# The first gate product of a gated MLP on rows without their norm

## The chip, the core and the metric

The kernel runs on one NeuronCore of a Trainium2 chip. Its engines work side by side and meet at semaphores: TensorE (PE, with PEld for its weight loads), VectorE (DVE), ScalarE (ACT), GpSimd (POOL) and SyncE (SP, which issues the transfers). The metric is the time of one execution in microseconds on the device.

## The reference, cut to what matters

Two layers of a diffusion backbone on 256 latent and 256 context tokens with 2048 channels. Every sub-layer normalises its input, scales and shifts it by a vector that depends on the condition, and adds its result to the stream. The part at hand is the gated MLP of the second layer (layer 1), which follows that layer's attention and has 5504 inner channels:

```python
def rms_norm(x, g):
    xf = x.astype(jnp.float32)
    y = xf * lax.rsqrt(jnp.mean(xf * xf, axis=-1, keepdims=True) + NORM_EPS)
    return (y * g.astype(jnp.float32)).astype(x.dtype)

def modulate(x, shift, scale):
    return x * (1 + scale) + shift

def conv_ffn(u, w_gate, w_up, conv_w, conv_b, w_down):
    T = u.shape[1]
    gp = jnp.pad(u @ w_gate, ((0, 0), (1, 1), (0, 0)))
    gte = gp[:, :T] * conv_w[0] + gp[:, 1:T + 1] * conv_w[1] + gp[:, 2:] * conv_w[2] + conv_b
    return (jax.nn.silu(gte) * (u @ w_up)) @ w_down
```

Here u is the normalised, scaled and shifted stream. The norm's factor is one number per token, and the shift is one number per channel.

## The kernel before, in words

Channels lie on the 128 partitions, so the stream `hl` is 16 tiles (index k) of 128 channels by 256 tokens. Products run in 32-bit numbers held as a pair of a rounded high half and a low half. `split` makes such a pair of a weight piece: ScalarE casts the high half (L148), VectorE or GpSimd subtracts to get the low one (L150). The inner channels are 43 tiles (index f) of 128. A product of one f, g for the gate and u for the other factor, is 16 matmuls of 512 columns, high weights on the high and low rows side by side (L1018), and 16 matmuls of 256 columns, low weights on the high rows (L1021); they come in two halves of eight k. Each product fills one of four PSUM banks with the tag "gu". `gate1` reads the banks of g and u (ScalarE's copy at L1029 and VectorE's addition at L1030, which make `eg`), applies the convolution and the gate, and so frees them.

Ahead of it stands the attention's output (`_attention`): sixteen products `op0` to `op15` of the rows `oA0` to `oA15`, each added to `hl` (L1363). The function gives back the last of these additions; `hold` is a list of instructions behind which later splits are ordered.

The fourth norm `n4` is between the two. `add` squares each tile of `hl` on ScalarE (L347) and sums the squares on VectorE; `totals` sums over channels by matmuls with one column (`n4s`, L366) and reduces on VectorE (L369, L370); GpSimd takes the power (L374); `spread` puts the factors on a diagonal (`n4d`, VectorE L380) and spreads them over all partitions by one matmul (`n4b`, L382). Then `norm_b` makes the row pairs `B0` to `B15`: VectorE multiplies (`nrmB`, L986), ScalarE adds the shift and rounds the high half (L987), and the low half comes from VectorE for even k (L993), and from a second ScalarE operation (L990) and GpSimd (L991) for odd k. M(1, 4, k, 0) is the scale vector of tile k, M(1, 3, k, 0) the shift.

The order of the instructions on each engine is not written by hand. It comes from a simulation of the program when it is built, under priorities (`urgent`, `high_priority`) and the `hold` list; tiles come from pools with a fixed number of buffers, three and three for the weight pairs, and an instruction that takes a buffer waits for the last reader of the tile that had it before.

Of the kernel before, what the change touches and what calls it, by code (L numbers as in the profile page):

```python
# [10 lines left out]
F32 = mybir.dt.float32  # L11
F32R = mybir.dt.float32r
AF = mybir.ActivationFunctionType
ALU = mybir.AluOpType
AX = mybir.AxisListType
PSUM = bass.MemoryType.PSUM

P = 128
D = 2048
KT = D // P  # L20
T = 256
# [39 lines left out]
def kernel(ctx: ExitStack, tc: tile.TileContext, xT, cxT, wmod, wg, wu, wd, wp,  # L61
                         wq, wv, wo, vec, cc, rope, inv, strips, out):
    nc = tc.nc
# [16 lines left out]
    def flat(a):  # L80
        return a.rearrange("p s t -> p (s t)")
# [25 lines left out]
    hold = []  # L107
# [46 lines left out]
    def ld(src, name, share=0):  # L154
        return split(load(lambda a, b: src[:, a:b], 2048, name), name, share)
# [178 lines left out]
    class Norm:  # L334
# [8 lines left out]
        def add(self, h_of, k):  # L343
            sq = self.pool.tile([P, 512], F32, tag="t2", name=f"{self.name}q{k}")
            with self.urgent(k):
                for s in self.streams:
                    nc.scalar.activation(sq[:, T * s : T * s + T], h_of(s)[:, k, :], AF.Square)  # L347
                if k >= KT - self.ends:
                    self.last.append(sq)
                elif self.acc is None:  # L350
                    self.acc = sq
                else:
                    nc.vector.tensor_tensor(self.acc[:, : self.n], self.acc[:, : self.n], sq[:, : self.n], op=ALU.add)  # L353
# [22 lines left out]
        def spread(self, v, js, pb):  # L376

            dg = self.pool.tile([P, 512], F32, tag="t2", name=f"{self.name}d{js[0]}")
            for i, j in enumerate(js):
                nc.vector.tensor_scalar(dg[:, P * i : P * i + P], ident, v[:, j : j + 1], None, op0=ALU.mult)  # L380
            n = P * len(js)
            nc.tensor.matmul(pb[:, :n], ones, dg[:, :n], start=True, stop=True)  # L382
            return pb
# [60 lines left out]
    with ExitStack() as ph0:  # L444
# [6 lines left out]
        def h_of(s):  # L451
            return hc if s else hl
# [510 lines left out]

    for _ in moves:
        pass
    tail = _attention(tc, ap0, bank, ld, A, M, hl, wq, wv, wo, rope, band, ident, v_first)

    with ExitStack() as ph2:
        f1 = ph2.enter_context(tc.tile_pool(name="f1", bufs=8, reuse_waits="tile"))
# [6 lines left out]
        n4 = Norm((0,), f1, "n4", 2)  # L976
        for k in range(KT):
            n4.add(h_lat, k)
        rstd = n4.each()[0]
        B = {}  # L980

        def norm_b(ks):
            for k in ks:
                a = ap0.tile([P, 2, 2, T], F32R, tag=f"A{k}", name=f"B{k}")[:, 0]
                y = f1.tile([P, 512], F32, tag="t2", name=f"nrmB{k}")[:, 0:T]
                nc.vector.scalar_tensor_tensor(y, hl[:, k, :], M(1, 4, k, 0), rstd[:, 0:T], op0=ALU.mult, op1=ALU.mult)  # L986
                nc.scalar.activation(a[:, 0], y, AF.Identity, bias=M(1, 3, k, 0))  # L987
                if k % 2:
                    z = f1.tile([P, 512], F32, tag="t2", name=f"nrmBz{k}")[:, 0:T]
                    nc.scalar.activation(z, y, AF.Identity, bias=M(1, 3, k, 0))  # L990
                    nc.gpsimd.tensor_tensor(a[:, 1], z, a[:, 0].bitcast(F32), op=ALU.subtract)  # L991
                else:
                    ins = nc.vector.scalar_tensor_tensor(a[:, 1], y, M(1, 3, k, 0), a[:, 0].bitcast(F32),  # L993
                                                         op0=ALU.add, op1=ALU.subtract)
                B[k] = a
                if k == 9:
                    hold[:] = [ins.ins]

        def gu1(f):
            res = []  # L1000
            pre = None
            if f == 0:
                pre = [load(lambda a, b: w[1, f][:, a:b], 2048, f"w{nm}1_{f}") for nm, w in (("g", wg), ("u", wu))]
                for q, ts in enumerate(pre):
                    first = split(ts[:1], f"w{q}1_{f}_0")
                    hold[:] = [tail]
                    pre[q] = first + split(ts[1:], f"w{q}1_{f}_1")
                    hold.clear()
                norm_b(range(KT))
            elif f == 2:  # L1010
                hold.clear()
            for q, (nm, wsrc) in enumerate((("g", wg), ("u", wu))):
                parts = pre[q] if pre else ld(wsrc[1, f], f"w{nm}1_{f}", 2 if f % 4 > 1 else 0)
                ps = bank("gu", f"{nm}1_{f}")
                for j, (hi, lo) in enumerate(parts):
                    for k in range(8 * j, 8 * j + 8):
                        c = P * (k % 8)
                        nc.tensor.matmul(ps, hi[:, c : c + P], flat(B[k]), start=(k == 0), stop=False)  # L1018
                    for k in range(8 * j, 8 * j + 8):
                        c = P * (k % 8)  # L1020
                        nc.tensor.matmul(ps[:, T:], lo[:, c : c + P], B[k][:, 0], start=False, stop=(k == KT - 1))  # L1021
                res.append(ps)
            return res

        def gate1(f, banks):
            res = []
            for nm, ps in zip("gu", banks):
                e = f1.tile([P, 512], F32, tag="t2", name=f"e{nm}_{f}")[:, 0:T]
                nc.scalar.copy(e, ps[:, T:])  # L1029
                nc.vector.tensor_tensor(e, e, ps[:, :T], op=ALU.add)  # L1030
                res.append(e)
            pg, pu = res
            g1 = f1.tile([P, 512], F32, tag="t2", name=f"g1b_{f}")[:, 0:T]
            nc.scalar.activation(g1, pg, AF.Identity, scale=V("cw1_1")[:, f : f + 1], bias=V("cb_1")[:, f : f + 1])
            nc.vector.scalar_tensor_tensor(g1[:, 1:T], pg[:, 0 : T - 1], V("cw0_1")[:, f : f + 1],
                                           g1[:, 1:T], op0=ALU.mult, op1=ALU.add)
            nc.vector.scalar_tensor_tensor(g1[:, 0 : T - 1], pg[:, 1:T], V("cw2_1")[:, f : f + 1],
                                           g1[:, 0 : T - 1], op0=ALU.mult, op1=ALU.add)
            sg = f1.tile([P, 512], F32, tag="t2", name=f"sgb_{f}")[:, 0:T]
            nc.scalar.activation(sg, g1, AF.Silu)  # L1040
            nc.vector.tensor_tensor(sg, sg, pu, op=ALU.mult)
            a = f1.tile([P, 2, T], F32R, tag="act", bufs=8, name=f"actb_{f}")
            nc.scalar.copy(a[:, 0], sg)  # L1043
            nc.vector.tensor_tensor(a[:, 1], sg, a[:, 0].bitcast(F32), op=ALU.subtract)  # L1044
            return a
# [99 lines left out]
def _attention(tc, ap0, bank, ld, A, M, hl, wq, wv, wo, rope, band, ident, v_first):  # L1145
# [9 lines left out]
    with ExitStack() as es:  # L1155
# [179 lines left out]
                prev = v, P * j  # L1335
        queue.append(attend(KT - 1, *prev))

        X = {}

        def x_tile(k):  # L1340
            a = ap0.tile([P, 2, 2, T], F32R, tag=f"A{k}", name=f"oA{k}")[:, 0]
            nc.scalar.copy(a[:, 0], O[k])
            nc.vector.tensor_tensor(a[:, 1], O[k], a[:, 0].bitcast(F32), op=ALU.subtract)
            X[k] = a
# [41 lines left out]
        for m in range(KT):  # L1386
# [6 lines left out]
                o_mm(ps, parts, ks, m == KT - 1)  # L1393
            with tc.high_priority() if m == KT - 1 else ExitStack():
                ins = o_end(ps, m)
        return ins


# [97 lines left out]
```

## Time and profile before

| what | value |
|---|---|
| three timed runs | 3042.36, 3039.24, 3041.61 us; median 3041.61 |
| profiled execution | 3042.44 us, its span 3040.7 us |
| mean granted clock of TensorE | 0.991 |
| PE, PEld busy | 98%, 79% of the span |
| DVE, ACT, POOL busy | 68%, 44%, 29% |
| attention's output stage | about 2219 to 2294 us |
| fourth norm and the first rows | 2294 to 2302 us |
| layer 1's gated MLP | 2302 to 3030 us |

The times in the trace count from the span's start. A row of a timeline gives the start, the length, the engine and line, the operation with output and inputs, the shapes, the number of like instructions, and in brackets the idle time just before with what ended it. A row of waits gives the engine and line that waited, the one it waited for, the sum, the count and the longest. A row of windows gives the busy times of the engines in a stretch, TensorE's granted clock as a share of full speed, the share of the transfer engines, and GB/s.

### The profile page before, as it was taken

The page shows a single profiled execution, that of the slowest core. Times are in us where ns is not written, and L with a number is a line of the kernel's source. Part 1 is how long each engine was busy: PE and PEld are TensorE (multiplying, and loading weights), DVE is VectorE, ACT ScalarE, POOL GpSimd, SP SyncE. Part 2 cuts the span into 40 slices and gives each one's busy share as a digit, 9 for nine tenths or more (in the row PEclk, how much of TensorE's full clock was granted, in tenths as well). Part 3 has the DMA queues.
Part 4 walks back from the last instruction along what each step waited for, and adds up shares of the span by engine and source line. Part 5 has one row for each costly group of instructions (what it writes and reads, how often), then busy time and mean ns, then how long its engine had stood idle before and what let it go on. Part 6 is the DMA issues. An engine that isn't in the chain of part 4 may idle for free.

```text
span 3040.7 us, 40895 instructions
## 1 busy us (share of the span) xinstructions
PE 2972.1 (98%) x14846; PEld 2399.2 (79%) x14846; DVE 2054.5 (68%) x2894; ACT 1347.4 (44%) x2205; POOL 884.4 (29%) x868
## 2 busy tenths in 40 slices
PE   6999999999999999999999999999999999999998
PEld 2565678887888888888887888888888888888887
DVE  5445887576876867587686666474867666666666
ACT  3333473323334232333334444343546666566665
POOL 1111320303213030322413111010102566566665
PEclk9999999999999999999999999999999999999999
DMA  9878635454866857676783333333355555555563
GB/s 376 326 279 322 218 97 171 157 185 157 254 195 193 260 174 243 201 235 205 215 240 101 112 109 109 103 113 104 112 165 181 180 192 191 192 181 189 183 195 113
DMA packets 224778, 572.31 MB, mean 188 GB/s; under 512 B 55232, under 2 KB 68032, under 8 KB 224576
## 3 DMA queue, kind: packets, MB, share of 16 engines
q1 hardware_dynamic: 224576, 569.70, 58.0%
q8 instruction: 117, 1.92, 0.3%
q14 instruction: 85, 0.70, 0.1%
HBM read 563.32 MB, written 11.53 MB: 189 GB/s over the span
## 4 chain that ended last, share of the span: by engine, by line
PE 89%; issue 3%; DVE 3%; DMA 2%; ACT 1%; POOL 1%; SPq 0%; DVEq 0%; ACTq 0%; POOLq 0%
PE g L1018 5%; PE u L1018 5%; PE d L900 5%; PE d L902 5%; PE d L901 5%; PE d L1068 4%; PE u L865 4%; PE u L863 4%; PE u L864 4%; PE g L865 4%; PE g L864 4%; PE g L863 4%; PE u L1021 3%; PE g L1021 3%; PE d L1072 2%
## 5 line engine op out<-in xcount | busy, mean ns | idle before, releaser
L921 POOL TENSOR_TENSOR hl<-hl,dy 128x256 f32<-128x256 f32 x144 | 146.2, 1015 | 941.8 <-ACT dy L918 676.8
L1085 POOL TENSOR_TENSOR hl<-hl,dy 128x256 f32<-128x256 f32 x320 | 327.1, 1057 | 188.5 <-ACT dy L1083 186.2
L270 DVE SCALAR_TENSOR_TENSOR macc<-wm,sc,macc 128x512 f32<-128x512 f32 x360 | 262.3, 780 | 9.0 <-DMA wm<-wmod 8.9
L248 DVE SCALAR_TENSOR_TENSOR macc<-wm,sc,macc 128x1024 f32<-128x1024 f32 x120 | 160.4, 1336 | 87.3 <-DMA wm<-wmod 86.1
L918 ACT ACTIVATE dy<-d,modT 128x256 f32<-128x256 f32 x224 | 93.6, 471 | 138.6 <-PE d L902 134.7
L921 POOL TENSOR_TENSOR hc<-hc,dy 128x256 f32<-128x256 f32 x144 | 141.4, 982 | 0.0
L1261 POOL COPY bias<-rows 128x160 f32<-128x160 f32 x64 | 37.1, 579 | 306.2 <-issue 195.6
L1083 ACT ACTIVATE dy<-d,modT 128x512 f32<-128x512 f32 x160 | 104.5, 684 | 42.8 <-PE d L1072 41.3
L184 PE MATMUL mod<-wm,sc 128*32 128x512 f32 x640 | 101.6, 616 | 21.2 <-DVE n1q L353 18.9
L150 DVE TENSOR_TENSOR wd_2l<-wd,wd_2h 128x1024 fp32r<-128x1024 f32 (+1 forms) x44 | 58.6, 1343 | 60.5 <-ACT wd_2h L148 60.5
L488 ACT ACTIVATE sg<-g 128x512 f32<-128x512 f32 x43 | 27.3, 634 | 146.0 <-DVE g L485 145.9
L150 DVE TENSOR_TENSOR wd_3l<-wd,wd_3h 128x1024 fp32r<-128x1024 f32 (+1 forms) x44 | 54.5, 1262 | 52.7 <-ACT wd_3h L148 52.7
L575 POOL TENSOR_TENSOR pf<-ws,inv 128x256 f32<-128x256 f32 x32 | 27.9, 894 | 204.4 <-DVE ws L567 131.9
L148 ACT CAST wd_0h<-wd 128x1024 fp32r<-128x1024 f32 (+1 forms) x44 | 45.3, 1032 | 79.5 <-PE g L864 51.0
L150 DVE TENSOR_TENSOR wd_1l<-wd,wd_1h 128x1024 fp32r<-128x1024 f32 (+1 forms) x44 | 55.3, 1259 | 31.6 <-ACT wd_1h L148 31.6
L184 PEld LDWEIGHTS mod<-wm,sc 128*32 128x32 f32 x640 | 18.4, 109 | 65.1 <-issue 32.7
L1044 DVE TENSOR_TENSOR actb<-sgb,actb 128x256 fp32r<-128x256 f32 x43 | 52.9, 1229 | 23.7 <-ACT actb L1043 23.7
L900 PE MATMUL d<-act,wd_0h 128*128 128x512 f32 x172 | 67.4, 395 | 1.0 <-ACT dy L918 1.0
L900 PE MATMUL d<-act,wd_3h 128*128 128x512 f32 x172 | 68.2, 396 | 0.0
L901 PE MATMUL d<-act,wd_2h 128*128 128x512 f32 x172 | 68.1, 396 | 0.0
L150 DVE TENSOR_TENSOR wd_0l<-wd,wd_0h 128x1024 fp32r<-128x1024 f32 (+1 forms) x44 | 53.8, 1226 | 21.0 <-ACT wd_0h L148 21.0
L902 PE MATMUL d<-act,wd_0l 128*128 128x512 f32 x172 | 67.9, 395 | 0.0
(1708 smaller groups left out, 9381.7 us busy)
## 6 DMA issues: line engine op xcount, KB each, us to landing
wm<-wmod SPq DMA_DIRECT2D x384, 512.0 KB, 6.2
wd<-wd SPq DMA_DIRECT2D x168, 512.0 KB, 4.5
wg<-wg SPq DMA_DIRECT2D x156, 512.0 KB, 4.6
wu<-wu SPq DMA_DIRECT2D x156, 512.0 KB, 4.5
wv<-wv SPq DMA_DIRECT2D x32, 512.0 KB, 3.7
wk<-wq SPq DMA_DIRECT2D x32, 512.0 KB, 3.7
wq<-wq SPq DMA_DIRECT2D x32, 512.0 KB, 3.7
wo<-wo SPq DMA_DIRECT2D x32, 512.0 KB, 4.4
```

The costliest lines, as they stand in the source:

```text
L150: eng.tensor_tensor(lo[:, :n], t[:, :n], hi[:, :n].bitcast(F32), op=ALU.subtract)
L270: nc.vector.scalar_tensor_tensor(acc[:, s], w, sc2[:, k, s : s + 1], acc[:, s], op0=ALU.mult, op1=ALU.add)
L863: nc.tensor.matmul(ps, hi[:, c : c + P], xh, start=(k == 0), stop=False)
L864: nc.tensor.matmul(ps, hi[:, c : c + P], xl, start=False, stop=False)
L865: nc.tensor.matmul(ps, lo[:, c : c + P], xh, start=False, stop=(k == KT - 1))
L900: nc.tensor.matmul(ps, hi[:, o : o + P], xh, start=(i == 0), stop=False)
L901: nc.tensor.matmul(ps, hi[:, o : o + P], xl, start=False, stop=False)
L902: nc.tensor.matmul(ps, lo[:, o : o + P], xh, start=False, stop=(i == n - 1))
L921: nc.gpsimd.tensor_tensor(h_of(s)[:, k, :], h_of(s)[:, k, :], y[:, s], op=ALU.add)
L1018: nc.tensor.matmul(ps, hi[:, c : c + P], flat(B[k]), start=(k == 0), stop=False)
L1021: nc.tensor.matmul(ps[:, T:], lo[:, c : c + P], B[k][:, 0], start=False, stop=(k == KT - 1))
L1085: nc.gpsimd.tensor_tensor(hl[:, k, :], hl[:, k, :], y[:, q], op=ALU.add)
```

## The change

The product is linear in its rows, so the norm's factor, which depends on the token alone, can be applied to the result, and the shift adds one number for each inner channel. The change does this for the first gate product, g1_0.

- For each k a raw row pair, `hl` times the scale without the factor and the shift, is made by one ScalarE operation (high half) and one VectorE operation (low half). It lies in the second half of the tile `oA{k}`, whose first half has the attention's rows. `norm_b` now writes the B pair into the first half of the same tile, so its tiles have the names `oA0` to `oA15` in the changed order.
- `sh` holds the shift vectors as high and low halves: four casts and four subtractions of 128x4.
- g1_0 is computed from the raw rows, ahead of `norm_b`.
- `shift_sums` multiplies the same weights with the shift: 32 matmuls of two columns into `gsh`, and one reduction.
- In the first `gate1` two operations more multiply by the factor and add `gsh`.
- The second half of the first u weights is split only after the last square (`n4.done`) and the diagonal (`n4.diag`), and the splits of the second pair of products after the last square.

```diff
-                    nc.scalar.activation(sq[:, T * s : T * s + T], h_of(s)[:, k, :], AF.Square)
+                    self.done = nc.scalar.activation(sq[:, T * s : T * s + T], h_of(s)[:, k, :], AF.Square).ins
...
+        raw = {}
+        for k in range(KT):
+            a = raw[k] = rows[k][:, 1]
+            with n4.urgent(k):
+                nc.scalar.activation(a[:, 0], hl[:, k, :], AF.Copy, scale=M(1, 4, k, 0))
+                nc.vector.scalar_tensor_tensor(a[:, 1], hl[:, k, :], M(1, 4, k, 0), a[:, 0].bitcast(F32),
+                                               op0=ALU.mult, op1=ALU.subtract)
+        sh = f1.tile([P, KT, 2], F32R, bufs=1, name="sh")
+        for k in range(0, KT, 4):
+            v = modT[1, 12 + k // 4][:, :, 0]
+            nc.scalar.copy(sh[:, k : k + 4, 0], v)
+            nc.vector.tensor_tensor(sh[:, k : k + 4, 1], v, sh[:, k : k + 4, 0].bitcast(F32), op=ALU.subtract)
         rstd = n4.each()[0]
...
-                a = ap0.tile([P, 2, 2, T], F32R, tag=f"A{k}", name=f"B{k}")[:, 0]
+                a = rows[k][:, 0]
...
-                    hold[:] = [tail]
+                    hold[:] = [tail] + [n4.done, n4.diag] * q
                     pre[q] = first + split(ts[1:], f"w{q}1_{f}_1")
                     hold.clear()
+                ps = bank("gu", "g1_0")
+                gu_b(ps, pre[0], raw)
+                shift_sums(pre[0])
+                res.append(ps)
                 norm_b(range(KT))
+                hold.append(n4.done)
...
+        def shift_sums(parts):
+
+            ps = bank("d", "gsh")
+            for k in range(KT):
+                c = P * (k % 8)
+                for j, w in enumerate(parts[k // 8]):
+                    nc.tensor.matmul(ps[:, 0:2], w[:, c : c + P], sh[:, k, :], start=(k == 0 and j == 0),
+                                     stop=(k == KT - 1 and j == 1))
+            nc.vector.tensor_reduce(out=gsh, in_=ps[:, 0:2], axis=AX.X, op=ALU.add)
...
+                if f == 0 and nm == "g":
+                    nc.vector.tensor_tensor(e, e, rstd[:, 0:T], op=ALU.mult)
+                    nc.vector.tensor_scalar(e, e, gsh, None, op0=ALU.add)
```

The matmuls of the products stand in a function `gu_b` of their own, at L1043 and L1046; otherwise they are as they were.

The order moves at three places. On TensorE, between the last output column and the first rows, there stood before:

```order
L1353 MATMUL op15_18584<-oA15_17950,wo15l1_18581 128x256
L366 MATMUL n4s_18687<-ones_72,n4q15_18685 128x1 x2
L382 MATMUL n4b0_18698<-n4d0_18699,ones_72 128x256
L1018 MATMUL g1_0_18823<-B0_18727,w01_0_0h0_18711 128x512
L1018 MATMUL u1_0_18856<-B0_18727,w11_0_0h0_18719 128x512
L1018 MATMUL g1_1_18917<-B0_18727,wg1_1h0_18909 128x512
```

Now, around n4s (`w01_0_0h0` and `w01_0_0l0` are the first half of g1_0's weights, `w01_0_1h0` and `w01_0_1l0` the second):

```order
L1043 MATMUL g1_0_18769<-oA13_17725,w01_0_1h0_18757 128x512
L1043 MATMUL g1_0_18769<-oA14_17943,w01_0_1h0_18757 128x512
L1056 MATMUL gsh_18802<-sh_18719,w01_0_0h0_18753 128x2
L366 MATMUL n4s_18728<-ones_72,n4q15_18685 128x1 x2
L1056 MATMUL gsh_18802<-sh_18719,w01_0_0l0_18754 128x2
L1056 MATMUL gsh_18802<-sh_18719,w01_0_0h0_18753 128x2
L1056 MATMUL gsh_18802<-sh_18719,w01_0_0l0_18754 128x2
L1043 MATMUL g1_0_18769<-oA15_17950,w01_0_1h0_18757 128x512
L1046 MATMUL g1_0_18769<-oA8_17710,w01_0_1l0_18758 128x256
```

So 23 of g1_0's 32 matmuls and the first of the 32 shift sums stand ahead of n4s; behind it come three shift sums, the other nine of g1_0 (of which two are shown), 22 shift sums, n4b, and the last six. After them u1_0, g1_1 and u1_1 take turns, one k each.

Further on TensorE, the fifth product g1_2 began before when the four ahead of it were through:

```order
L1021 MATMUL u1_1_18962<-B13_18804,wu1_1l1_18959 128x256
L1021 MATMUL u1_1_18962<-B14_18811,wu1_1l1_18959 128x256
L1021 MATMUL u1_1_18962<-B15_18816,wu1_1l1_18959 128x256
L1018 MATMUL g1_2_19023<-B0_18727,wg1_2h0_19015 128x512
L1018 MATMUL g1_2_19023<-B1_18732,wg1_2h0_19015 128x512
```

Now it begins after k = 12 of the other three:

```order
L1043 MATMUL u1_0_18916<-oA12_17722,w11_0_1h0_18765 128x512
L1043 MATMUL g1_1_18979<-oA12_17722,wg1_1h1_18975 128x512
L1043 MATMUL u1_1_19024<-oA12_17722,wu1_1h1_19020 128x512
L1043 MATMUL g1_2_19085<-oA0_17686,wg1_2h0_19077 128x512
L1043 MATMUL g1_2_19085<-oA1_17689,wg1_2h0_19077 128x512
```

Its first matmul takes the bank of g1_0 and stands behind the gate's addition that makes eg_0.

On ScalarE the rows of B and the gate's copy have moved. Before, the copy of the first gate stood right behind the cast of wu1_2's second half:

```order
L148 CAST wu1_1h1_18958<-wu1_1_1024_18952 128x1024
L148 CAST wu1_2h1_19064<-wu1_2_1024_19058 128x1024
L1029 COPY eg_0_18889<-g1_0_18823 128x256
```

Now five row operations, for k = 13 to 15, lie between them:

```order
L148 CAST wg1_2h1_19081<-wg1_2_1024_19075 128x1024
L148 CAST wu1_2h1_19126<-wu1_2_1024_19120 128x1024
L999 ACTIVATE oA13_17725<-nrmB13_18900,modT1_86 128x256
L1002 ACTIVATE nrmBz13_18903<-nrmB13_18900,modT1_86 128x256
L999 ACTIVATE oA14_17943<-nrmB14_18906,modT1_86 128x256
L999 ACTIVATE oA15_17950<-nrmB15_18910,modT1_86 128x256
L1002 ACTIVATE nrmBz15_18913<-nrmB15_18910,modT1_86 128x256
L1064 COPY eg_0_18949<-g1_0_18769 128x256
```

On VectorE the low halves of `wg1_1` stand behind the low half of row 8, as before; now SyncE issues wu1_2's two transfers behind them.

More of the change, by code (lines that the diff above doesn't have):

```diff
@@ L379, in spread @@
             for i, j in enumerate(js):
-                nc.vector.tensor_scalar(dg[:, P * i : P * i + P], ident, v[:, j : j + 1], None, op0=ALU.mult)
+                self.diag = nc.vector.tensor_scalar(dg[:, P * i : P * i + P], ident, v[:, j : j + 1], None, op0=ALU.mult).ins
             n = P * len(js)
@@ L965 @@
         pass
-    tail = _attention(tc, ap0, bank, ld, A, M, hl, wq, wv, wo, rope, band, ident, v_first)
+    tail, rows = _attention(tc, ap0, bank, ld, A, M, hl, wq, wv, wo, rope, band, ident, v_first)
     with ExitStack() as ph2:
@@ L1012, in gu1, with gu_b @@
             for q, (nm, wsrc) in enumerate((("g", wg), ("u", wu))):
+                if f == 0 and q == 0:
+                    continue
                 parts = pre[q] if pre else ld(wsrc[1, f], f"w{nm}1_{f}", 2 if f % 4 > 1 else 0)
                 ps = bank("gu", f"{nm}1_{f}")
[L1015 to L1021, printed above, removed]
+                gu_b(ps, parts, B)
                 res.append(ps)
             return res
+        def gu_b(ps, parts, x):
+            for j, (hi, lo) in enumerate(parts):
+                for k in range(8 * j, 8 * j + 8):
+                    c = P * (k % 8)
+                    nc.tensor.matmul(ps, hi[:, c : c + P], flat(x[k]), start=(k == 0), stop=False)
+                for k in range(8 * j, 8 * j + 8):
+                    c = P * (k % 8)
+                    nc.tensor.matmul(ps[:, T:], lo[:, c : c + P], x[k][:, 0], start=False, stop=(k == KT - 1))
+        gsh = main.tile([P, 1], F32, name="gsh")
+        def shift_sums(parts):
+            ps = bank("d", "gsh")
+            for k in range(KT):
+                c = P * (k % 8)
+                for j, w in enumerate(parts[k // 8]):
+                    nc.tensor.matmul(ps[:, 0:2], w[:, c : c + P], sh[:, k, :], start=(k == 0 and j == 0),
+                                     stop=(k == KT - 1 and j == 1))
+            nc.vector.tensor_reduce(out=gsh, in_=ps[:, 0:2], axis=AX.X, op=ALU.add)
         def gate1(f, banks):
@@ L1336, in _attention @@
         queue.append(attend(KT - 1, *prev))
-        X = {}
+        X, rows = {}, {}
         def x_tile(k):
-            a = ap0.tile([P, 2, 2, T], F32R, tag=f"A{k}", name=f"oA{k}")[:, 0]
+            rows[k] = ap0.tile([P, 2, 2, T], F32R, tag=f"A{k}", name=f"oA{k}")
+            a = rows[k][:, 0]
             nc.scalar.copy(a[:, 0], O[k])
@@ L1395, in _attention @@
                 ins = o_end(ps, m)
-        return ins
+        return ins, rows
 def _cm(v):
```

## The prediction

> **What bounds the kernel now.** I read the page's first and fourth parts, then TensorE's waits around the change, then the timeline there, then windows on both sides of it.
>
> ```profile
> PE 2972.1 (98%) x14846; PEld 2399.2 (79%) x14846; DVE 2054.5 (68%) x2894; ACT 1347.4 (44%) x2205; POOL 884.4 (29%) x868
> PE 89%; issue 3%; DVE 3%; DMA 2%; ACT 1%; POOL 1%; SPq 0%; DVEq 0%; ACTq 0%; POOLq 0%
> ```
>
> TensorE works 98% of the span and carries 89% of the chain that ended last. Only idle or slow time on TensorE can be won. From 2290 to 3030 us it waits here:
>
> ```profile
> PE n4b L382 <- DVE n4d L380: 2.4, 1, 2.4
> PE g L1018 <- DVE B L993: 2.2, 1, 2.2
> PE n4s L366 <- ACT n4q L347: 1.4, 1, 1.4
> ```
>
> These are the three steps of the fourth norm: 2.37 + 2.24 + 1.38 = 5.99 us by the timeline below. That is all the idle time the change can fill.
>
> ```profile
> 2293.57 0.28 PE L1353 MATMUL op<-oA,wo15l 128*128 128x256 f32 x1
> 2295.23 0.67 PE L366 MATMUL n4s<-ones,n4q 128*128 128x1 f32 x4 [1.38 <-ACT n4q L347]
> 2298.26 1.22 PE L382 MATMUL n4b<-n4d,ones 128*128 128x256 f32 x2 [2.37 <-DVE n4d L380]
> 2301.72 0.76 PE L1018 MATMUL g<-B,w_0h 128*128 128x512 f32 x1 [2.24 <-DVE B L993]
> ...
> 2305.27 0.63 PE L1018 MATMUL g<-B,wg_1h 128*128 128x512 f32 x1
> 2305.70 0.48 PE L1018 MATMUL g<-B,w_0h 128*128 128x512 f32 x1
> ...
> 2326.02 0.86 PE L1018 MATMUL g<-B,wg_2h 128*128 128x512 f32 x3
> ```
>
> The row at 2326.02 is the first matmul of the fifth product; ahead of it lie the four products g_0, u_0, g_1, u_1. I compare the two kernels there, because behind it TensorE has no gap at all:
>
> ```profile
> 2296.00:2302.00 6.00, 1.50 (x3) 0.81 (x4) 3.84 (x12) 1.96 (x5) 1.27 (x2) 0.50 0.54 176
> 2302.00:2306.00 4.00, 4.00 (x10) 3.10 (x10) 4.00 (x11) 4.00 (x11) 2.38 (x4) 0.52 0.00 0
> 2306.00:2310.00 4.00, 4.00 (x23) 3.44 (x22) 4.00 (x6) 2.35 (x6) 3.65 (x2) 1.00 0.32 100
> ...
> 2400.00:2600.00 200.00, 200.00 (x1147) 175.60 (x1146) 135.21 (x131) 123.30 (x180) 130.09 (x108) 1.00 0.59 190
> 2600.00:3020.00 420.00, 420.00 (x2435) 370.03 (x2433) 284.30 (x283) 264.91 (x390) 281.42 (x241) 1.00 0.56 178
> ```
>
> After the length, the columns are the busy time of PE, PEld, DVE, ACT and POOL, then the granted clock. TensorE is busy 200.00 of 200 and 420.00 of 420, so a shift at 2326 carries to the end unchanged. The first rows show a second cost: the clock stood at 0.50 through the gap and 0.52 until 2306, so the first products ran slow.
>
> **Prices of a product.**
>
> ```profile
> 2284.07 2.00 PE L1355 MATMUL op<-oA,wo14h 128*128 128x512 f32 x8
> 2285.91 1.11 PE L1359 MATMUL op<-oA,wo14l 128*128 128x256 f32 x8
> 2286.87 0.28 PE L1351 MATMUL op<-oA,wo15h 128*128 128x256 f32 x1
> ```
>
> From start to start at full clock, eight 512-column matmuls take 1.84 (0.23 each) and eight of 256 take 0.96 (0.12). A product of 16 + 16 takes 5.60. In the slow clock the pitch of a large one is 2305.70 − 2305.27 = 0.43, or 0.20 lost each. From 2301.72 to 2306 there are some 9.5 of them: 1.9 us lost. Check: 4 × 5.60 + 1.9 = 24.3 = 2326.02 − 2301.72.
>
> **Step 1: g_0 moved ahead.** No product is removed; g_0 goes into the gap. The last output column ends its issue at 2293.57 + 0.12 = 2293.69. By the order, 23 products of g_0 (8 large, 8 small, 7 large: 4.4 us) and one shift-sum product stand ahead of n4s, so n4s goes out at 2298.2, not 2295.23. The wait of 1.38 is covered, and the norm's own chain starts 3 us later.
>
> **Step 2: the shift sums.** 32 products of two columns are new. The trace has no such matmul; the nearest are the one-column norm sums.
>
> ```profile
> 1661.55 2.83 PE L366 MATMUL n3s<-ones,n3q 128*128 128x1 f32 x24
> 351.14 0.95 PE L366 MATMUL n2s<-ones,n2acc 128*128 128x1 f32 x8
> ```
>
> That is 0.118 and 0.119 per matmul with the tail of the last in it. I take 0.11, which makes 3.5 us in all, with 0.06 (hidden weight loads) and 0.13 as ends: 1.9 to 4.2. The Trainium skill, TensorE: Matmul & The Clock Gate, section Back-to-back issue gap, puts matmuls of 1 to 64 columns at about 25 ns; it would make the 32 an estimated 0.8 us. The rows, which include a weight load for each, are four times that, and I keep to the rows.
>
> **Step 3: the chain of the norm.**
>
> ```profile
> 2296.55 0.16 DVE L369 TENSOR_REDUCE n4v<-n4s 128x2 f32<-128x6 f32 x1
> 2296.74 0.17 DVE L370 TENSOR_SCALAR n4v<-n4v 128x2 f32<-128x2 f32 x1
> 2297.73 0.48 DVE L380 TENSOR_SCALAR n4d<-ident,n4v 128x128 f32<-128x128 f32 x2 [0.81 <-POOL n4v L374]
> 2299.52 1.66 DVE L986 SCALAR_TENSOR_TENSOR nrmB<-hl,modT,n4b 128x256 f32<-128x256 f32 x4 [1.31 <-PE n4b L382]
> 2300.04 0.91 ACT L987 ACTIVATE B<-nrmB,modT 128x256 fp32r<-128x256 f32 x2 [4.87 <-DVE nrmB L986]
> 2301.10 0.48 DVE L993 SCALAR_TENSOR_TENSOR B<-nrmB,modT,B 128x256 fp32r<-128x256 f32 x1
> ...
> 2302.28 0.48 DVE L993 SCALAR_TENSOR_TENSOR B<-nrmB,modT,B 128x256 fp32r<-128x256 f32 x1
> ```
>
> From the reduction to the end of the diagonal it takes 2297.73 + 0.48 − 2296.55 = 1.66. After n4s at 2298.2 and some 0.55 for its result, n4d is ready at 2300.4. TensorE meanwhile has 3 tiny products, one large and 8 small of g_0, and 22 tiny ones (0.3 + 0.2 + 1.0 + 2.4): it reaches n4b at about 2302.4 without a wait. The 2.37 is gone.
>
> **Step 4: from the broadcast to the first normalised row.** This stays open. Before, it was 2301.72 − 2298.26 = 3.46. I take 0.35 off (n4b at full clock) and put 0.16 on (the shift sum's reduction, as the reduction at 2296.55, ahead of oA0's low half on VectorE): 3.3. Only six tiny products are left to fill it, so some 2 us idle remain. TensorE goes on at 2305.7 with g_0 done; before, it had reached that amount at 2301.72 + 5.60 = 2307.3. Ahead by 1.6.
>
> **Step 5: the clock.** From 2299.9 to 2305.7 TensorE has only tiny products, n4b and idling. The third norm shows what such a stretch does:
>
> ```profile
> 1661.00:1664.00 3.00, 3.00 (x27) 2.73 (x25) 1.26 (x3) 1.90 (x4) 0.00 (x0) 1.00 0.03 11
> 1664.00:1667.00 3.00, 1.14 (x6) 0.91 (x6) 1.30 (x6) 0.00 (x0) 1.39 (x2) 0.53 0.00 0
> ```
>
> Three microseconds full of one-column products did not hold it: the clock then read 0.53. So I take the same 1.9 us of slow products as before; that cancels, between a gain of 1.9 (stays full) and a loss of 1.3 (3.2 us slow, by where the gap falls). The same page of the skill, section Why this matters for your kernels, allows idle gaps up to about 3 us; the idle time left is 2 us, and by that the clock would stay full. By the n3 rows it does not.
>
> **Step 6: the new wait.** In the changed order u_0, g_1 and u_1 go forward together and the fifth product, g1_2, begins after thirteen large and eight small of each. It takes the PSUM bank of g1_0, which the gate must read first. On ScalarE the gate's copy stands behind the cast of wu1_2's second half and five row operations; that cast waits for a transfer, which SyncE issues when VectorE is through with the low halves of wg_1.
>
> ```profile
> 2306.21 2.35 DVE L150 TENSOR_TENSOR wg_1l<-wg,wg_1h 128x1024 fp32r<-128x1024 f32 x2
> 2319.86 1.05 ACT L148 CAST wu_2h<-wu 128x1024 fp32r<-128x1024 f32 x1
> 2320.80 0.36 ACT L1029 COPY eg<-g 128x256 f32<-128x256 f32 x1
> 2321.28 0.41 DVE L1030 TENSOR_TENSOR eg<-eg,g 128x256 f32<-128x256 f32 x1
> wu<-wu SPq DMA_DIRECT2D x2, 512.0 KB, 4.5
> ```
>
> Row 0's low half begins 0.62 ahead of the first product, at 2305.1; four pairs of rows at 2302.28 − 2301.10 = 1.18 and one low half bring 2310.3; wg_1l at 2.35 less the overlap of its two, 2312.6; the transfer 4.5, 2317.1; the cast 0.9, 2318.0; five row operations at 0.41 (0.91 for two, less the tail), 2320.0; copy and addition 0.9, 2320.9. TensorE gets there after 39 large and 24 small (11.85) and the 1.9 of step 5: 2319.4. It waits 1.5 us.
>
> **Step 7: work that costs nothing.** ScalarE gets 16 raw rows and VectorE 16 low halves (some 0.45 and 0.48 each, by the B rows). All but the last lie in the attention's output stage:
>
> ```profile
> 2280.00:2294.00 14.00, 13.85 (x99) 12.78 (x97) 7.26 (x12) 7.74 (x10) 0.00 (x0) 1.00 0.62 202
> ```
>
> VectorE is free for 6.7 of 14 us there and ScalarE for 6.3; a column of 16 + 16 takes TensorE 5.60, and the added 0.93 for each fits. If that cover were gone, the columns' ends would hold PSUM banks and TensorE would wait. The eight tiny shift operations and the two more operations of the first gate (some 0.4 each, the first ahead of nothing that TensorE awaits) hide likewise. The last raw row, ready after n4q15, is needed only as g_0's 24th large product.
>
> **Sum at the fifth product.** 2320.9 plus what is left of u_0, g_1 and u_1 (9 large, 24 small: 4.95) is 2325.85, against 2326.02: 0.2 us sooner. The profiled execution took 3042.44 (its span 3040.7 and 1.7 around it), 0.8 above the median of the three runs; on the median 3041.61 this gives 3041.4.
>
> **The rivals.**
> - *No wait for the bank, and a full clock* (for it: the transfer may land sooner than 4.5, and the idle rest is short; against: the n3 rows). Then step 4's 1.6 stays and 1.9 of slow products come on top: 3.5 sooner, 3038. Where only the bank is free in time, 1.6 sooner, 3040. With tiny products at 0.06 the n4b comes 1.3 sooner and the end with it, 3040.
> - *The bank is the bound* (slower). The chain of step 6 has one transfer in it, and the page's slowest kind shows what one can take:
>
> ```profile
> wm<-wmod SPq DMA_DIRECT2D x384, 512.0 KB, 6.2
> ```
>
>  With 6.2 in place of 4.5 the wait is 3.2 and the end 1.5 later: 3043.1. It decides against the change once the wait passes 1.7. For it: three queues in a row; against: the copy is 0.36 and could go earlier only by the order, which is fixed.
> - *Raw rows on the path* (slower). If VectorE and ScalarE could not take the 16 × 0.93 = 14.9 us beside the columns, half of it uncovered would be 7.5: 3049. Against: the free 6 us of 14 above. It becomes measurable at about 6.4 uncovered.
> - *The change does nothing.* Excluded, since the order shows g_0 ahead of n4s.
>
> **How the numbers follow.** My forecast with its neighbours (0.5 sooner to 0.5 later) 0.5; free bank, warm clock or cheap products 0.27; bank as the bound 0.17; raw rows 0.06. All but the last lie within 0.2% (6.1 us), which is about what a measurement can tell from no change. Faster by more needs all 5.99 of idling, the 1.9 and cheap tiny products together (7.9 − 1.9 = 6.0): 0.04. The range runs from the first rival's 3038 to the bank's 3043.1, each with the 1.3 by which the runs shown spread about their middle: 3036.7 to 3044.4.
>
> **What would show it right or wrong.** Right: TensorE's wait for n4d is gone, a wait of about 2 us for oA0's low half stays, the clock reads about 0.5 around 2303 to 2308, and a new wait of g1_2 on the gate's addition of g1_0 appears. Wrong: no such wait, or a start of the fifth product's amount of work more than 3 us from 2326; tiny products at a pitch of 0.06; waits of TensorE for the output columns ahead of 2293.

## The result, and the profile after

| | before | changed |
|---|---|---|
| median | 3041.81 us (8 runs) | 3048.10 us (8 runs) |
| lowest and highest | 3038.97, 3043.51 | 3044.34, 3051.48 |
| ratio, 95% interval | | 1.0021 [1.0012, 1.0030] |
| profiled span | 3040.7 | 3049.1 |

The changed kernel is 6 us slower, outside the forecast's range (3036.7 to 3044.4). Beside the experiments below it ran again: 3046.62 against 3042.26, ratio 1.0018 [1.0009, 1.0026].

TensorE's busy share is as before; what counts is where it waits behind the output stage (engine and line that waited, what it waited for, sum, count, longest):

```profile
PE 2977.6 (98%) x14878; PEld 2403.3 (79%) x14878; DVE 2056.8 (67%) x2917; ACT 1354.4 (44%) x2225; POOL 881.3 (29%) x868
PE u L1043 <- DVE oA L1005: 5.2, 3, 2.0
PE g L1043 <- DVE eg L1065: 1.5, 1, 1.5
```

The waits for n4s and n4b are gone. In their place stand three waits for the low half of a row, one of which (for row 0) was forecast, and the one for g1_0's bank, forecast at 1.5. TensorE's timeline shows where:

```profile
2294.20 0.28 PE L1392 MATMUL op<-oA,wo15l 128*128 128x256 f32 x1
...
2298.75 0.58 PE L366 MATMUL n4s<-ones,n4q 128*128 128x1 f32 x4
...
2303.18 0.68 PE L382 MATMUL n4b<-n4d,ones 128*128 128x256 f32 x2
...
2306.84 0.77 PE L1043 MATMUL u<-oA,w_0h 128*128 128x512 f32 x1 [1.94 <-DVE oA L1005]
...
2319.88 0.73 PE L1043 MATMUL u<-oA,w_1h 128*128 128x512 f32 x2 [1.25 <-DVE oA L1005]
...
2323.51 0.50 PE L1043 MATMUL u<-oA,w_1h 128*128 128x512 f32 x1 [1.98 <-DVE oA L1005]
...
2326.05 3.75 PE L1043 MATMUL g<-oA,wg_2h 128*128 128x512 f32 x8 [1.47 <-DVE eg L1065]
```

Row 0 is waited for at 2306.84, row 10 at 2319.88, row 12 at 2323.51; g1_2 gets its bank at 2326.05, and its first eight matmuls take 3.55 us instead of 1.84 (the next row of the timeline begins at 2329.60). The granted clock (the column behind the five engines) was at half twice, not once:

```profile
2306.00:2310.00 4.00, 3.16 (x8) 2.52 (x9) 3.79 (x10) 4.00 (x11) 2.02 (x3) 0.50 0.01 4
...
2326.00:2330.00 4.00, 3.95 (x10) 3.21 (x11) 0.71 (x2) 0.12 (x1) 0.00 (x0) 0.50 0.32 129
```

Why the rows are late stands on VectorE, with GpSimd and ScalarE beside it:

```profile
2311.59 2.89 DVE L150 TENSOR_TENSOR wg_1l<-wg,wg_1h 128x1024 fp32r<-128x1024 f32 x2
2314.80 2.51 DVE L150 TENSOR_TENSOR wu_1l<-wu,wu_1h 128x1024 fp32r<-128x1024 f32 x2
2317.62 2.21 DVE L1005 SCALAR_TENSOR_TENSOR oA<-nrmB,modT,oA 128x256 fp32r<-128x256 f32 x1
2319.75 1.21 DVE L150 TENSOR_TENSOR wg_2l<-wg,wg_2h 128x1024 fp32r<-128x1024 f32 x1
2320.88 2.58 DVE L1005 SCALAR_TENSOR_TENSOR oA<-nrmB,modT,oA 128x256 fp32r<-128x256 f32 x1
```

```profile
2316.88 2.66 POOL L150 TENSOR_TENSOR wg_2l<-wg,wg_2h 128x1024 fp32r<-128x1024 f32 x1 [1.79 <-ACT wg_2h L148]
2320.73 2.44 POOL L150 TENSOR_TENSOR wu_2l<-wu,wu_2h 128x1024 fp32r<-128x1024 f32 x1 [1.20 <-ACT wu_2h L148]
```

```profile
2319.61 1.05 ACT L148 CAST wu_2h<-wu 128x1024 fp32r<-128x1024 f32 x1 [3.19 <-DMA wu<-wu]
2323.89 0.91 ACT L999 ACTIVATE oA<-nrmB,modT 128x256 fp32r<-128x256 f32 x2 [2.42 <-DVE nrmB L998]
2325.10 0.35 ACT L1064 COPY eg<-g 128x256 f32<-128x256 f32 x1
```

Two pairs of weight halves (5.4 us) stand ahead of row 10's low half, and one more half ahead of row 12's. The two low halves, 0.48 to 0.66 for the five rows in front of them, take 2.21 and 2.58: each begins beside a GpSimd operation on 128x1024 and ends within 0.3 us of its end (2319.54, 2323.17). ScalarE waits for VectorE's next rows until 2323.89, so the copy that frees the bank comes at 2325.10.

The profile before had shown such a stretch a little further on: one weight half on VectorE, 1.21 to 1.23 elsewhere, took 3.09 beside a GpSimd operation that ended at 2325.64.

```profile
2323.62 3.09 DVE L150 TENSOR_TENSOR wg_3l<-wg,wg_3h 128x1024 fp32r<-128x1024 f32 x1
2322.57 3.07 POOL L150 TENSOR_TENSOR wu_2l<-wu,wu_2h 128x1024 fp32r<-128x1024 f32 x1 [5.14 <-ACT eu L1029]
```

**A ruler for all runs.** Since executions differ by some microseconds long ahead of this place, I measure two lengths in each profile: the stage, from the last matmul of op15 to the first of g1_4, and the rest, from there to the first of u1_40. Between the same points lie the same products.

```profile
2348.37 0.86 PE L1018 MATMUL g<-B,wg_4h 128*128 128x512 f32 x3
2958.21 1.09 PE L1018 MATMUL u<-B,wu_40h 128*128 128x512 f32 x4
```

```profile
2355.80 1.55 PE L1043 MATMUL g<-oA,wg_4h 128*128 128x512 f32 x6
...
2966.66 1.55 PE L1043 MATMUL u<-oA,wu_40h 128*128 128x512 f32 x6
```

The first two rows are of before: the stage is 2348.37 − 2293.57 = 54.80 and the rest 609.84. The second pair is of the changed kernel: 2355.80 − 2294.20 = 61.60, and 610.86. So the stage lost 6.8 in this execution, and the rest 1.0 more. All profiles by this ruler (rests that differ by 0.01 are put as one), with the ratio of the times (its 95% interval) where the kernel was timed several times:

| kernel | stage, us | rest, us | ratio to before |
|---|---|---|---|
| before, two profiles | 54.80, 55.36 | 609.84 each | |
| changed, three profiles | 61.60, 57.99, 57.84 | 610.86 each | 1.0021, again 1.0018 |
| bank read early | 53.94 | 610.86 | 1.0002 [0.9994, 1.0011] |
| rows first | 54.07 | 610.86 | 1.0008 [0.9999, 1.0017] |
| GpSimd's pieces on VectorE, two profiles | 56.25 each | 610.86 | 1.0021 [1.0012, 1.0030] |
| no shift sums | 58.13 | 610.86 | 1.0005 [0.9996, 1.0014] |
| raw rows alone | 55.80 | 610.86 | 1.0011 [1.0002, 1.0020] |
| order mended | 50.99 | 610.86 | 0.9991 [0.9982, 1.0000] |
| large products in the gap | 51.07 | 610.86 | 0.9986 [0.9977, 0.9995] |
| the same, other addresses | 50.69 | 607.16 | 0.9977 [0.9968, 0.9986] |
| before, 4 bytes more | 54.81 | 609.84 | |
| before, 128 bytes more | 55.22 | 610.86 | |
| before, 192 bytes more | 54.13 | 607.16 | 0.9991 [0.9982, 1.0000] |

### The profile page after: what moved, and what is told of

It is laid out like the page before. It is cut to its first block, busy times and chain, and to the rows that moved or that the text cites. A ratio compares the mean times of both kernels' runs of the same rounds, so it can differ in the third digit from the quotient of the medians.

```text
span 3049.1 us, 41014 instructions
## 1 busy us (share of the span) xinstructions
PE 2977.6 (98%) x14878; PEld 2403.3 (79%) x14878; DVE 2056.8 (67%) x2917; ACT 1354.4 (44%) x2225; POOL 881.3 (29%) x868
## 5 line engine op out<-in xcount | busy, mean ns | idle before, releaser
L488 ACT ACTIVATE sg<-g 128x512 f32<-128x512 f32 x43 | 27.3, 634 | 150.8 <-DVE g L485 150.7
L902 PE MATMUL d<-act,wd_2l 128*128 128x512 f32 x172 | 67.9, 395 | 0.0
L900 PE MATMUL d<-act,wd_1h 128*128 128x512 f32 x172 | 67.9, 395 | 0.0
```

The costliest lines, as they stand in the source:

```text
L900: nc.tensor.matmul(ps, hi[:, o : o + P], xh, start=(i == 0), stop=False)
L902: nc.tensor.matmul(ps, lo[:, o : o + P], xh, start=False, stop=(i == n - 1))
```

## The experiments

**Bank read early.** g1_0's bank is copied out right behind the shift sums, into a buffer of its own.

```diff
                 shift_sums(pre[0])
-                res.append(ps)
+                eg0 = f1.tile([P, T], F32, bufs=1, name="eg0")
+                nc.scalar.copy(eg0, ps[:, T:])
+                nc.vector.tensor_tensor(eg0, eg0, ps[:, :T], op=ALU.add)
+                res.append(eg0)
...
```

> g1_0's bank is read (one ScalarE copy, one VectorE addition into a buffer of its own) right behind the shift sums instead of behind the row operations; nothing else of the change is altered. Theory 1 (late rows): the rows 10 and 12 are late because VectorE makes low halves of weights first and its row operations stretch beside GpSimd; then VectorE's low halves of rows 10 and 12 come as late as in the changed kernel (2.21 and 2.58 us long), but TensorE may fill the time with g1_2: the 1.47 for the bank is gone, the 1.25 and 1.98 for the rows shrink to under 1.5 together, and the time falls by 3 to 6 us, to 3042 to 3045. Theory 2 (the bank alone is the loss): all of it comes back, 3040 or less. Theory 3 (the loss is the shift sums or lies outside this stage): under 1.5 us come back.

TensorE's only wait behind the output stage, what it does at 2312, and row 10's low half on VectorE beside GpSimd's piece:

```profile
PE u L1046 <- DVE oA L1005: 2.0, 1, 2.0
```

```profile
2312.00 1.79 PE L1046 MATMUL g<-oA,wg_2h 128*128 128x512 f32 x7
```

```profile
2312.01 2.49 DVE L1005 SCALAR_TENSOR_TENSOR oA<-nrmB,modT,oA 128x256 fp32r<-128x256 f32 x1
```

```profile
2311.82 2.40 POOL L150 TENSOR_TENSOR wg_2l<-wg,wg_2h 128x1024 fp32r<-128x1024 f32 x1 [2.35 <-ACT wg_2h L148]
```

Row 10 is still late by the same stretch (2.49; its low half ends 25.5 us behind the last column, in the changed kernel 25.6), yet TensorE waits for row 0 alone: with the bank free it works on g1_2 meanwhile. The stage is 53.94, 0.9 to 1.4 under before, where the prediction's first rival put a free bank 1.6 under it. The time is 3042.05, in the range that theory 1 gave.

**Rows first.** The splits of the next weights are held behind row 14's low half, the last on VectorE, not behind row 8's.

```diff
-                if k == 9:
+                if k == 15:
                     hold[:] = [ins.ins]
```

> The low halves of the weights of g1_1, u1_1 and g1_2 are held behind the low half of row 14 on VectorE, not of row 8; so all rows are made first, and the copy that reads g1_0's bank stands behind the rows but ahead of g1_2's cast. Theory 1 (late rows): TensorE's waits of 1.25 and 1.98 for rows 10 and 12 vanish, so does the 1.47 for the bank, and the second slow stretch of the clock behind them; the wait of about 2 us for row 0 stays. The fifth product's amount of work is then reached about 1 us before that of the kernel before (counted from the last output column): 3040 to 3042. Theory 2 (the bank): the same, since the bank is free in time too. Theory 3 (shift sums, or outside this stage): stays at 3046 to 3048.

```profile
PE u L1043 <- DVE oA L1005: 1.9, 1, 1.9
```

Again only row 0 is waited for; the stage is 54.07, the median 3042.64. Either edit alone undoes the loss of the stage. So it takes both: rows late behind weights, and a TensorE that has nothing else to do because the next product's bank is locked by work that stands behind those rows on ScalarE.

**GpSimd's pieces on VectorE.** The second pieces of g1_2 and u1_2 get their low halves on VectorE.

```diff
-                parts = pre[q] if pre else ld(wsrc[1, f], f"w{nm}1_{f}", 2 if f % 4 > 1 else 0)
+                parts = pre[q] if pre else ld(wsrc[1, f], f"w{nm}1_{f}", 2 if f % 4 > 1 and f > 2 else 0)
```

> The low halves of the second pieces of g1_2 and u1_2 are made by VectorE, behind row 12 and row 15, instead of by GpSimd; the order on VectorE up to row 12's low half is as in the changed kernel. Theory 1a (VectorE's row operations stretch because GpSimd works on a 128x1024 piece): the low halves of rows 10 and 12 take 0.48 us each instead of 2.21 and 2.58, TensorE's waits for them fall from 1.25 and 1.98 to under 0.3 and under 0.5, and 2 to 5 us come back. Theory 1b (they are long for another reason, such as a wait on a semaphore counted as busy): 2.2 and 2.6 us stay, and so does the time.

> The version with the low halves of g1_2's and u1_2's second pieces on VectorE, for a second profile, since its profile showed the stage 5 us shorter than the first one of the changed kernel and its times showed nothing of it. Theory 1a (GpSimd's piece stretches VectorE's row operations): again 0.5 us for rows 10 and 12 and no wait for the bank, with the stage ending 1 to 2 us later than in the kernel before. If the stage ends 3 us or more later this time, the gain in the first profile was an accident.

Row 10's and row 12's low halves, and TensorE's waits:

```profile
2315.83 0.47 DVE L1005 SCALAR_TENSOR_TENSOR oA<-nrmB,modT,oA 128x256 fp32r<-128x256 f32 x1
...
2317.36 0.47 DVE L1005 SCALAR_TENSOR_TENSOR oA<-nrmB,modT,oA 128x256 fp32r<-128x256 f32 x1
```

```profile
PE u L1043 <- POOL oA L1003: 2.1, 1, 2.1
PE u L1043 <- DVE oA L1005: 2.0, 1, 2.0
```

The stretch is gone: 0.47 each, in the same place of VectorE's order. That theory 1a is right about the stretch is shown; row 13, behind a cast that waits for a transfer, is then late instead (2.1). The stage is 56.25 in two profiles, 1.6 to 5.4 under the changed kernel; part of this can come from TensorE's order, in which g1_2 now begins behind all of u_0, g_1 and u_1. The timed runs do not show the gain (1.0021, as the changed kernel), and this stays unexplained. The two profiled executions (3044.10, 3043.84) lie under the median of the ten timed ones (3046.95), so the profiles may show less than the usual loss.

**The changed kernel again.**

> The changed kernel once more, on the chip and beside the runs of the others here, for a second profile. Theory A (late rows on VectorE, and TensorE locked out of g1_2 by the bank): the same three waits of TensorE, 1 to 2.5 us each, for rows 10, 12 and the bank of g1_0, and a second slow stretch of the clock behind them; 4 to 6 us above the kernel before. Theory B (the loss in the first profile was an accident of one execution): other waits, and within 2 us of the kernel before.

> The changed kernel for a third profile, since its stage was 6.6 us longer than before's in the first and 3.1 in the second. If the slow clock behind the waits sets the difference: the stage is near 3 us longer where the first product of g1_2 runs at full clock, near 6 where it runs at half; the three waits of TensorE for rows 10 and 12 and for the bank, or two of them, are there in either case. Another size or other waits: open.

Of the second profile:

```profile
PE u L1043 <- DVE oA L1005: 3.5, 2, 1.9
PE g L1043 <- DVE eg L1065: 2.0, 1, 2.0
```

```profile
2324.07 2.10 PE L1043 MATMUL g<-oA,wg_2h 128*128 128x512 f32 x8 [1.99 <-DVE eg L1065]
```

Row 0, row 10 and the bank are waited for, not row 12 (its low half takes 0.47 this time), and g1_2's first eight matmuls run near full clock (1.94). The third profile has the same (sums 3.4 and 2.0). So in two of three profiles the stage loses about 3 us, and the first, on which the comparison above rests, had 3.7 more: row 12 stretched, so that the bank came 1.4 later (counted from the last column), and from the bank to g1_4 it took 29.75 instead of 27.47 and 27.46, with the second slow stretch of the clock. Theory A holds for row 10, the bank and the time (4.4 above before); the wait for row 12 and the second slow stretch, which it also expected, were of the first profile alone.

**No shift sums.** The 32 tiny products, their reduction and their addition are left out; the shift is missing from the first gate product.

```diff
-                shift_sums(pre[0])
...
-                    nc.vector.tensor_scalar(e, e, gsh, None, op0=ALU.add)
```

> The changed kernel without the 32 shift sums, their reduction and the addition of their result (the shift is left out of the first gate product). Theory A: the norm's broadcast and the rows come about 2 us sooner, but the order on VectorE still puts low halves of weights ahead of rows 10 to 15 and the gate's copy behind rows 13 to 15, so TensorE still waits for rows and for the bank, 2 to 5 us in all; the time falls by 1.5 to 3 us against the changed kernel and stays above the kernel before. Theory C (the 32 tiny products are the loss): it falls by 5 us or more, to the kernel before or under it.

```profile
PE g L1042 <- DVE eg L1064: 2.6, 1, 2.6
PE u L1042 <- DVE oA L1005: 2.5, 1, 2.5
PE u L1042 <- POOL oA L1003: 1.2, 1, 1.2
```

```profile
2322.73 3.75 PE L1042 MATMUL g<-oA,wg_2h 128*128 128x512 f32 x8 [2.62 <-DVE eg L1064]
```

Counted from the last column, TensorE has row 0 2.7 to 3.0 us sooner, and the bank comes at 28.0, where the changed kernel has it at 30.4 to 31.9. TensorE still waits for the bank, and longer (2.62), since it gets there sooner. This profile has the slow stretch behind the wait (3.75 in the row): from the bank to g1_4 it takes 30.15, against 27.46 and 27.47 in the two profiles of the changed kernel without such a stretch. Its execution was the slowest of its eleven, so its stage (58.13) is no measure of the gain. The median fell by 4.2, to 3042.41 (ratio to before 1.0005), which lies between theory A's 1.5 to 3 and theory C's 5. So the wait for the bank does not hang on the tiny products, but they delay the rows and the bank alike, and leaving them out brings back about as much of the time as either edit of the order. The forecast had them in its sum (step 2); they are no part of what it missed.

**Raw rows alone.** The raw rows and shift halves are made and not used; g1_0 runs on B rows as before.

```diff
...
-                ps = bank("gu", "g1_0")
-                gu_b(ps, pre[0], raw)
-                shift_sums(pre[0])
-                res.append(ps)
                 norm_b(range(KT))
...
```

> The kernel before with the raw rows and the shift's halves made beside it (16 + 4 more operations on ScalarE and 16 + 4 on VectorE, in the second half of the attention's row tiles), but g1_0 computed as before; nothing reads them. Theory A: they lie beside TensorE's work in the output stage; TensorE's waits for n4s, n4b and row 0 stay at 1.4, 2.4 and 2.2 us with at most 1 us more (the last raw row behind the last square), and the time within 1.5 us of the kernel before. Theory D (the raw rows are the loss): 3 us or more above it, with waits for output columns ahead of 2293 us.

```profile
PE n4b L382 <- DVE n4d L380: 2.8, 1, 2.8
PE g L1036 <- DVE oA L1005: 2.2, 1, 2.2
PE n4s L366 <- ACT n4q L347: 1.4, 1, 1.4
```

No output column waits. The last raw row stands ahead of the norm's reduction on VectorE and costs 0.46 at n4b. The stage is 0.4 to 1.0 longer, and the rest 1.0; the ratio 1.0011 [1.0002, 1.0020] allows for that. Theory D falls, though the raw rows were not quite free.

**Order mended.** Rows first, bank early, n4s behind the first half of g1_0 and the shift sums behind n4b.

```diff
...
-                gu_b(ps, pre[0], raw)
-                shift_sums(pre[0])
+                gu_b(ps, pre[0], raw, n4.sums)      # second half behind the last n4s matmul
+                with tc.issue_after(n4.cast):       # behind n4b
+                    shift_sums(pre[0])
...
```

> The changed kernel with four edits of order: the norm sums n4s stand behind the first half of g1_0 (not behind 23 products), the 32 shift sums behind n4b, g1_0's bank is read early, and the rows come before the low halves of g1_1 and later on VectorE. By theory 1 nothing is left that waits: n4s 2.8 us behind the last output column, n4b 5.8, row 0 ready about 9.4 to 9.8, where the shift sums end at 9.4; TensorE's waits for n4b and row 0 under 0.5 together, none for rows 10 and 12 and for the bank; the slow clock may still cost about 2 us, since 3.5 us of shift sums come before the first product. Against the kernel before about 3.5 to 4.5 us: 3037 to 3038.5. By theory 3 not under 3043.

TensorE waits for nothing here; its first product behind the tiny ones, and the windows:

```profile
2302.09 0.52 PE L1048 MATMUL u<-oA,w_0h 128*128 128x512 f32 x1
```

```profile
2300.00:2304.00 4.00, 4.00 (x25) 3.67 (x26) 3.67 (x10) 4.00 (x9) 1.48 (x2) 0.80 0.31 108
2304.00:2308.00 4.00, 4.00 (x15) 3.11 (x15) 3.61 (x9) 4.00 (x11) 1.77 (x3) 0.77 0.00 0
```

The stage is 50.99, 3.8 under before; the time 3038.68, with a ratio whose interval just reaches 1. The clock still fell, with TensorE busy all the time by its records.

**Large products in the gap.** The second half of g1_0 behind n4b, 16 shift sums ahead of n4b and 16 behind the product.

```diff
-                gu_b(ps, pre[0], raw, n4.sums)
+                gu_b(ps, pre[0], raw, n4.cast)
...
+                with tc.issue_after(n4.sums if k < 8 else n4.cast):
```

> The last version of order, with the second half of g1_0 behind n4b and half of the shift sums ahead of it (16 behind n4s, 16 behind g1_0), so that large products stand in the stretch that was filled with 32 tiny ones. Theory A: no wait of TensorE from the last output column on, and the clock stays at full speed to the first products (or is slow for under 1 us): 1 to 2 us less than that version's 3038.7, so 3036.5 to 3038. If 16 tiny products bring the slow clock as well: no gain over it.

```profile
2298.00:2302.00 4.00, 4.00 (x22) 3.42 (x22) 3.19 (x9) 2.86 (x5) 0.70 (x1) 0.81 0.32 102
...
2306.00:2330.00 24.00, 24.00 (x136) 20.96 (x137) 22.05 (x29) 16.74 (x29) 12.12 (x8) 1.00 0.58 193
```

Behind the first sixteen tiny products the clock is slow as well (0.81), and the stage (51.07) is no shorter. The other sixteen, from 2304.26 to 2305.96, are followed by a full clock (1.00), so sixteen do not bring it each time. The time, 3038.0, is under before (0.9986).

**Addresses.** Behind the stage every kernel so far with the raw rows lost 1.0 us, evenly over 600 us. The change's new tiles, `gsh` (4 bytes on each partition) and `sh` (128), had moved other tiles, so four runs move tiles and leave the order as it was, but for one memset in three of them.

```diff
+        gsh = f1.tile([P, 16], F32, bufs=1, name="gsh")[:, 0:1]                    # best4
+        nc.vector.memset(main.tile([P, 1], F32, name="gap"), 0.0)                  # pad
+        nc.vector.memset(f1.tile([P, 32], F32, bufs=1, name="gap"), 0.0)           # fpad128; fpad192: 48
```

> The kernel before once more, for a second profile. In every profile of a changed kernel the products behind the gap run a little slower than in the one profile of before (large matmuls 0.2311 us apart instead of 0.2306, a drift of about 1.0 us from 2400 to 3000 us). Theory E (a new 4-byte tile moves weights and rows by 32 bytes, and that changes the pace): 0.2306 again. Theory F (an accident of that one execution): 0.2311.

> The kernel before with one more tile of 4 bytes a partition (a single memset on VectorE ahead of the fourth norm), which moves the weights' pairs, the rows and the gate's tiles by 32 bytes, as the tile for the shift sum does; the order of the instructions is as before but for that memset. Theory E: 0.2311 between large matmuls of a product in layer 1, and a drift of about 1.0 us from 2400 to 3000 us. Theory F: 0.2306 and no drift.

> The version with large products in the norm's gap, in the same order, but with the shift sum's tile moved behind the gate's tiles, so that weights and rows lie where they lay before. Theory E: the drift of about 1.0 us is gone (0.2306 between large matmuls), the stage as in that version (about 3.8 us ahead of the kernel before): 3037 or about 5 us under the kernel before. Theory F: as that version, about 4 us under.

> The kernel before with one more tile of 128 bytes a partition in the gate's pool (and a memset of it): the gate's tiles behind it and one of the two groups of weight buffers lie 128 bytes further from the rows, the distance they have in the changed kernel. Theory G (the pace of TensorE hangs on where these buffers lie against the rows): a drift of 0.9 to 1.1 us between 2400 and 3000 us against the kernel before, and about 0.2311 between large matmuls. Theory H (it comes with the raw rows or another part of the change): no drift, 0.2306.

> The same with 192 bytes, the distance (but for whole multiples of 256) of the fastest version. Theory G: about 2.6 us gained between 2400 and 3000 us with about 0.2295 between large matmuls, and 2 to 3.5 us less than the kernel before, without any part of the change. Theory H: no drift, and the time of the kernel before.

The points of the ruler in the kernel before with 128 bytes more, and with 192:

```profile
2350.48 1.79 PE L1019 MATMUL g<-B,wg_4h 128*128 128x512 f32 x7
...
2961.34 2.00 PE L1019 MATMUL u<-B,wu_40h 128*128 128x512 f32 x8
```

```profile
2346.92 1.99 PE L1019 MATMUL g<-B,wg_4h 128*128 128x512 f32 x8
...
2954.09 2.00 PE L1019 MATMUL u<-B,wu_40h 128*128 128x512 f32 x8
```

610.86 and 607.17, with the order of before, against its 609.84. With 4 bytes more, which move weights and rows together, it stays 609.84, so theory E as stated fell. With 128 bytes more in the gate's pool, as many as `sh` takes there, it is that of the changed kernel: what counts is where the gate's tiles and one group of weight buffers lie against the rest (theory G). The two were not moved apart, and moving everything by 128 bytes was not tried. The run that was to lie as before (best4) missed for the same reason: but for multiples of 256 it had 192 bytes more there, and it came out at 50.69 and 607.16, and 3036.03 us: 0.9977 [0.9968, 0.9986], the fastest of all. About 2.7 of its 7 us come from the addresses and are to be had without the change (0.9991 for 192 bytes alone).

## Why the prediction was wrong, step by step

- **Steps 1 to 3 held.** Counted from the last column's last matmul, n4s came at 4.55 in both of the first two profiles (forecast 4.6) and n4b at 8.98 and 8.99 (forecast 8.8).
- **Step 2's price held**: 0.11 apart in the timeline.
- **Step 4** forecast the restart at 12.1 by the same count; it came at 12.6 and 13.0, as ScalarE's row 0 stands behind a cast that waits for the last tiny product (VectorE then waited 0.33 for ScalarE's half of row 0).
- **Step 5 held in the first slow stretch**, and left out the second that a wait behind it can bring. Its rows of the third norm could not tell tiny products from idling behind them (TensorE was busy for 1.14 of 3.00 us where the clock read 0.53); the version with the mended order can.
- **Step 6 is the step that failed**, by the size of its sum. The mechanism was right: g1_2 waited for g1_0's bank, behind the cast, behind the transfer, behind VectorE. But the bank came at 30.5 and 30.4 in two profiles and at 31.9 in the first, where the chain was summed to 27.3. In the two profiles the 3.1 that were missing lie all along it: VectorE began row 0's low half 0.7 and 0.9 late; it ended wg_1l 1.5 and 1.6 late, 0.5 of this since wg_1l took 2.89 for 2.35; the cast began 2.6 late, as it came 5.5 and 5.6 behind wg_1l, where the transfer was put at 4.5; and row 14's low half, 1.5 beside GpSimd, made the rest. In the first profile the cast was only 1.9 late, but the copy then waited for rows behind row 12's stretched low half, for 2.6 more. The rows for VectorE were ones in which it lost nothing to GpSimd: beside the 2.35, GpSimd's two operations were the ones that gave way (3.65 for the two, 0.74 for one alone). So the rival "the bank is the bound" was the case, at about twice the price that I gave it, and the slower transfer on which it rested is only about a third of it. The wait named for the bank is just 1.5 to 2.0, since TensorE has already lost as much to row 10 in front of it.
- **Also in step 6**: rows 10 and 12 were not walked through VectorE's queue. The order showed two pairs of weight halves ahead of row 10's low half. Before, the second piece of wu_1 was cast only at 2318.90, behind a product that held its buffer; with g1_0 gone early the buffers come free early, and the low halves stand ahead of the rows. That the early buffers are the reason for the order is argued from this, not tried.
- **Step 7** left out what moves with a new tile: 1.0 us over the rest, and 0.3 in the attention ahead (from the first matmul of wk1 to that of wo0 455.94 for 455.62, and 455.94 too in the kernel before with 4 bytes more).
- By the ruler the sum is: the stage 2.5 to 3.2 longer (6.8 in the first profile) where 0.2 shorter was forecast, the rest 1.0, the attention 0.3: 3.8 to 8, where the two timings gave 6.3 and 4.4.

Where the stretch comes from is named in the Trainium skill, SBUF — State Buffer, section Who interferes with whom: VectorE and GpSimd share one pair of ports, which is an exclusive lock, and a VectorE instruction with two inputs in SBUF contends with a GpSimd instruction that reads SBUF. The trace agrees (0.47 without, 2.21 and 2.58 with a GpSimd operation beside it, which it outlives by 0.3). I had this rule at hand and priced VectorE's rows without it.

## What to carry to other kernels

When a product is moved ahead to fill a gap, follow not only what it frees but what it frees early: buffers that come free sooner let other work into the queues ahead of the rows that TensorE needs next. A bank that is read late locks out the very work that could cover such lateness; read it as soon as it is full. And price VectorE's queue by rows that lost to a GpSimd operation beside them where one will stand there, not by quiet ones; the profile before had such a row (3.09).

## What the runs showed of the hardware

- Busy by the records is not the same as a full clock. With TensorE busy in all of 2300 to 2308 the granted clock was 0.80 and 0.77, behind 32 matmuls of two columns; behind 16 of them it was 0.81, behind 16 more 1.00. The Trainium skill, TensorE: Matmul & The Clock Gate, section Why this matters for your kernels, speaks of idle gaps over about 3 us; here there was none, and the measurement decides.
- Where the gate's tiles and a group of weight buffers lie changes TensorE's pace: 609.84, 610.86 or 607.16 us for the same 600 us of products, the same to 0.01 in every profile of one placing. The three placings differ by 128 and 192 bytes; why one is faster is open.
